# New places in SBUF for the activations and the split weights of a two-layer decoder trunk

## The chip, the core and the metric

The kernel runs on one NeuronCore of a Trainium2 chip. The metric is the time of one execution on the device in microseconds (us), as the median of several runs; less is better. The engines are called as the profile calls them: PE is TensorE's matmul side, PEld its side that loads weights, DVE is VectorE, ACT is ScalarE, POOL is GpSimd, SP is SyncE, which here issues all loads.

## The reference

Two layers, each on 256 rows of width 2048, all in float32:

```
u  = rms_norm(x);  z = u @ W_in          # 2048 -> 512 | 576 | 2048 | 2048 | 2048 | 2048
A  = latent attention, 16 heads, causal  # from the first two parts
R  = gelu(y) * rg_lru(conv4(x_b))        # from the next two
x += (sigmoid(g_a)*A + sigmoid(g_r)*R) @ W_out
x += relu(rms_norm(x) @ W_up)^2 @ W_down # 2048 -> 8192 -> 2048
x += sigmoid(rms_norm(x) @ W_pg) * (p @ W_pe)
```

and a last RMS norm. Nearly all arithmetic is in the dense products; W_up and W_down are the largest.

## The kernel before, in words

**Layout.** Features lie on the 128 partitions, the 256 rows of the sequence along the free dimension. `x` is [128, 16, 256]. The two big activation buffers `bufA` and `bufB` are [128, 16, 2, 256]: for each of 16 feature tiles a high and a low part of 256 values, 1024 bytes each.

**Weights.** The host lays all weights out as halves of [128, 1024] float32. `load` fetches a half into one of six `raw` buffers; `split_half` makes of it a rounded `hi` (ACT) and a remainder `lo` (DVE), both float32r, 4096 bytes in a partition. Three halves are held at a time: the pool `wsp` has three buffers for `hi` and three for `lo`, used in turn.

**Products.** Each product of two float32 numbers is made of three matmuls: hi times high part, hi times low part, lo times high part. `mm_both` walks 4 feature tiles of a half for two output tiles (24 matmuls per half), `mm_half` 8 feature tiles for one output tile (24 as well). In nearly all of them the 128x128 weights block is loaded anew before each matmul and 256 columns of the activations stream through. So PE's queue is an endless row of pairs, a load of 128 columns of weights and a matmul of 256 columns.

**Stages of a layer.** First the projections `c` and `kr`; then eight groups of two heads, each with `xb`, `yb`, `k`, `v`, `q`, `qr`, `lru`, `gr`, scores `s`, transposes `pt`, values `o`, and `ga`; then `out`; then four chunks of `up` and `down`, the MLP; then `pp` and `pg`. In `k`, `q`, `qr` and `lru` the moving operand is a smaller activation tile (`c0`, `c1`, `xc`); in `v` such a tile is the stationary operand and the split weights stream; in `s` and `o` both are small tiles.

**What sets the order.** One Python pass (`half`, `work`, `later`, `need`) writes the order of every engine out, from its own table of costs. The order does not depend on addresses.

**Addresses.** Pools are laid out one behind another in the order in which they are opened, each tile rounded up to 32 bytes; the first one begins at byte 16,512 of a partition. By the byte's remainder on division by 512 the tiles before stand so: `x`, `bufA`, `bufB`, `ident`, `ones` at 128; `raw`, `hi`, `lo`, the `tmp` tiles and `PT` at 192, in all buffers alike; the tiles of the pool `att` that are allocated behind `xbuf` (`c0`, `c1`, `k`, `q`, `v`, `xc`, `kr`, `qs` and others) at 224, since `xbuf` takes 2080 bytes. Blocks inside these tiles follow at multiples of 512 bytes. So 128 and 192 are multiples of 64, and 224 is a multiple of 32 alone.

Of the kernel before, what the change touches and what calls it, by code (L numbers as in the profile page):

```python
# [11 lines left out]
F32 = mybir.dt.float32  # L12
F32R = mybir.dt.float32r
# [5 lines left out]
P = 128  # L19
S = 256  # L20
D = 2048
KT = D // P
DEPTH = 2
# [21 lines left out]
NPC = _c  # L45
# [8 lines left out]
def _parts(x, bits, n):  # L54

    out = []
    x = Fraction(x)
    for i in range(n):
        if x == 0:
            out.append(0.0)  # L60
            continue
        b = bits if i < n - 1 else 24
        m, e = math.frexp(float(x))
        q = Fraction(2) ** (e - b)
        v = Fraction(round(x / q)) * q
        out.append(float(v))
        x -= v
    return out


def _centered(x):
    x = x - math.floor(x)
    return x - 1 if x > Fraction(1, 2) else x
# [3 lines left out]
def trunk_kernel(ctx: ExitStack, tc: tile.TileContext, xT, pT, pos, par, gfin, invf, wu, out):  # L77
    nc = tc.nc

    const = ctx.enter_context(tc.tile_pool(name="const", bufs=1))  # L80
    wraw = ctx.enter_context(tc.tile_pool(name="wraw", bufs=6))
    wsp = ctx.enter_context(tc.tile_pool(name="wsp", bufs=3))
    tmp = ctx.enter_context(tc.tile_pool(name="tmp", bufs=6))
    att = ctx.enter_context(tc.tile_pool(name="att", bufs=1))
    tiny = ctx.enter_context(tc.tile_pool(name="tiny", bufs=4))
    banks = {
        t: (ctx.enter_context(tc.tile_pool(name=f"ps_{t}", bufs=n, space=PSUM)), n)
        for t, n in (("mm", 3), ("s", 2), ("t", 1), ("o", 1), ("r", 1))
# [4 lines left out]
    def f(ap):  # L93
        return ap.bitcast(F32)
# [50 lines left out]
    def load_to(h):  # L145
        while nxt["dma"] <= min(h, n_halves - 1):
            load(nxt["dma"])
            nxt["dma"] += 1
# [6 lines left out]
    def split_half(h):  # L155
        load_to(h)
        src = raws.pop(h)
        hi = wsp.tile([P, 1024], F32R, tag="hi", name=f"hi{h}")
        lo = wsp.tile([P, 1024], F32R, tag="lo", name=f"lo{h}")
        A.activation(hi, src, AF.Copy)  # L160

        E["A"] = max(E["A"], E["P"]) + 0.95
        work(E["A"] + LATENCY - 0.3, E["A"])
        V.tensor_tensor(out=lo, in0=src, in1=f(hi), op=ALU.subtract)  # L164
        E["V"] = max(E["V"], E["A"] + LATENCY) + 1.14
        halves[h] = (hi, lo, E["V"] + LATENCY)
# [42 lines left out]
    def later(key, *steps, deps=(), rank=1, also=()):  # L209

        job = Job((key, *also), rank, deps, steps)
        at = len(jobs)
        while at and jobs[at - 1].rank > rank:
            at -= 1
        jobs.insert(at, job)
# [11 lines left out]
    def work(until_v, until_a):  # L227
        until = {"V": until_v, "A": until_a, "G": until_v}
        while True:
            best = None  # L230
            for j in jobs:
                at = j.start()
                if at is None:
                    continue
                eng = j.steps[0][0]
                idle = at - E[eng]
                if at < until[eng] and (idle < 0.02 or at < E["P"] + STALL) and (best is None or idle < best[0] - 0.02):
                    best = (idle, at, j)
                    if idle < 0.02:
                        break  # L240
            if best is None:
                return
            best[2].step(best[1])

    def half():
        h = nxt["used"]
        nxt["used"] += 1
        while nxt["half"] <= min(h + min(LA, max(h - 1, 0)), n_halves - 1):
            split_half(nxt["half"])
            nxt["half"] += 1  # L250
        load_to(h + PD)
        work(E["P"] + WINDOW + 0.9, E["P"] + WINDOW)
        hi, lo, at = halves.pop(h)
        E["P"] = max(E["P"], at)
        return hi, lo
# [86 lines left out]
        return tmp.tile([P, S], F32, tag="h", bufs=3, name=name)  # L342


    x = const.tile([P, KT, S], F32, name="x")

    bufA, bufB = (const.tile([P, KT, 2, S], F32R, name=n) for n in ("bufA", "bufB"))
    parT = const.tile([P, DEPTH * NPC], F32, name="parT")
    gf = const.tile([P, KT], F32, name="gf")
    nc.sync.dma_start(out=parT, in_=par)  # L350
    nc.sync.dma_start(out=x[:, 0:2, :], in_=xT[:, 0:2, :])
    load_to(0)
# [12 lines left out]
    make_identity(nc, ident)  # L365
    ones = const.tile([P, P], F32, name="ones")
    V.memset(ones, 1.0)
    power = const.tile([P, 4], F32, name="power")
    A.activation(power, ones[:, 0:4], AF.Copy, scale=-0.5)
    mask = const.tile([P, S], F32, name="mask")  # L370
    V.memset(mask[:, 0:P], 0.0)
# [2 lines left out]
    ropeS = const.tile([P, S], F32, name="ropeS")  # L374

    def rope_tables():
        fr = const.tile([P, 1], F32, name="invf")
        nc.sync.dma_start(out=fr, in_=invf)
        slots = []
        for n, tag in enumerate(("xch", "xcl", "vh", "vl")):  # L380
            w = att.tile([P, 512], F32, tag=tag, name=f"rope_w{n}")
            slots += [w[:, 0:S], w[:, S:512]]
        posi, ang, p2, p1, rem, turn, k, k2 = slots
        nc.sync.dma_start(out=posi.bitcast(I32), in_=pos.partition_broadcast(P))
        ops = []

        def ts(*a, **kw):
            ops.append(("V", 0.21, lambda: V.tensor_scalar(*a, **kw)))

        def tt(*a, **kw):  # L390
            ops.append(("V", 0.35, lambda: V.tensor_tensor(*a, **kw)))

        def rounded(o, src, by):
            ts(out=o, in0=src, scalar1=by, scalar2=ROUND, op0=ALU.mult, op1=ALU.add)
            ts(out=o, in0=o, scalar1=ROUND, scalar2=None, op0=ALU.subtract)

        def less(o, src, kk, c):
            ops.append(("V", 0.35, lambda: V.scalar_tensor_tensor(out=o, in0=kk, scalar=-c, in1=src, op0=ALU.mult, op1=ALU.add)))

        ops.append(("V", 0.21, lambda: V.tensor_copy(ang, posi.bitcast(I32))))  # L400
        ts(out=ang, in0=ang, scalar1=fr, scalar2=None, op0=ALU.mult)

        rounded(p2, ang, 2.0 ** -20)
        less(rem, ang, p2, 2.0 ** 20)
        rounded(p1, rem, 2.0 ** -10)
        less(rem, rem, p1, 2.0 ** 10)
        for n, (p, e) in enumerate(((p2, 20), (p1, 10))):
            c = _parts(_centered(Fraction(2) ** e / (2 * _PI)), 12, 3)
            if n == 0:
                ts(out=turn, in0=p, scalar1=c[0], scalar2=None, op0=ALU.mult)  # L410
            else:
                less(turn, turn, p, -c[0])
            rounded(k, turn, 1.0)
            less(turn, turn, k, 1.0)
            less(turn, turn, p, -c[1])
            less(turn, turn, p, -c[2])
        rounded(k, turn, 1.0)
        less(turn, turn, k, 1.0)
        c = _parts(2 * _PI, 12, 3)
        rounded(k2, rem, float(1 / (2 * _PI)))  # L420
        for v in c:
            less(rem, rem, k2, v)
        less(rem, rem, turn, -float(2 * _PI))
        rounded(k, rem, float(1 / (2 * _PI)))
        for v in c:
            less(rem, rem, k, v)
        ts(out=k, in0=rem, scalar1=3.1415925, scalar2=-3.1415925, op0=ALU.min, op1=ALU.max)

        ts(out=k2, in0=k, scalar1=-1.0, scalar2=None, op0=ALU.mult)
        tt(out=k2, in0=k, in1=k2, op=ALU.max)  # L430
        ts(out=k2, in0=k2, scalar1=-1.0, scalar2=math.pi / 2, op0=ALU.mult, op1=ALU.add)
        ops.append(("A", 1.0, lambda: A.activation(ropeS, k, AF.Sin)))
        ops.append(("A", 1.0, lambda: A.activation(ropeC, k2, AF.Sin)))

        for b in (0, 64):
            ts(out=ropeS[b:b + 32, :], in0=ropeS[b:b + 32, :], scalar1=-1.0, scalar2=None, op0=ALU.mult)
        later("rope", *ops, rank=1)


    cl = const.tile([P, DEPTH, 16], F32, name="cl")  # L440
    cl2 = const.tile([P, DEPTH, 16], F32, name="cl2")
    hba = const.tile([P, DEPTH, 16], F32, name="hba")
    hbx = const.tile([P, DEPTH, 16], F32, name="hbx")

    def lru_constants():
        work_ = t512("lru_c")
# [196 lines left out]

    PT = tuple(att.tile([P, 512], F32R, name=f"pt_{w}") for w in ("hi", "lo"))

    xbuf = att.tile([P, 2, 260], F32, name="xbuf")
    V.memset(xbuf[:, :, 0:4], 0.0)

    def split_steps(d, name, src, tag, cols=512):
# [35 lines left out]
    def mixer(l, u, mg, norm):  # L685
# [9 lines left out]
        for n in range(4):  # L695
            i, pr = divmod(n, 2)
            key = ("c", i, pr, l)
            ps = mm_pair(f"c{i}{pr}_{l}", key, u, hooks.get(n, ()))
            later(key, ("A", 0.6, lambda i=i, pr=pr, ps=ps: A.activation(dest(i, pr), ps, AF.Copy)), rank=-1)
            if l == n == 0:  # L700
                rope_tables()
                lru_constants()
            nl.squares((nl.name, "sq", n), lambda i=i, pr=pr: raw[i, pr], i, deps=(key,), last=pr == 1)
# [729 lines left out]
```

## Time and profile before

| what | value |
|---|---|
| median of 2 runs | 2882.11 us (2880.01 to 2884.22) |
| the profiled execution | 2881.91 us, of which 2880.1 us are the span of the profile |
| PE | 2853.1 us busy, 99% of the span, 24,800 matmuls |
| PEld | 2846.8 us busy, 99%, 24,800 loads of weights |
| DVE, ACT | 1861.3 us (65%) and 1538.4 us (53%) |
| DMA | 535.43 MB, mean 186 GB/s |

A matmul's duration in the profile reaches from its start to the end of its last column, and the next one starts long before that; what a stream of matmuls costs is read from the distance of their starts, which is called the pace below.

### The profile page before, as it was taken

What the parts mean: (1) busy time and instruction counts of PE and PEld (TensorE: products, weight loads), DVE (VectorE), ACT (ScalarE), POOL (GpSimd) and SP (SyncE); (2) the same over time, 40 slices, a digit from 0 to 9 for tenths busy, and PEclk for the clock granted to TensorE, in tenths of its full rate; (3) what the DMA queues carried; (4) which work ended last, traced back from release to release, by engine and by line L of the source; (5) the groups of instructions that cost most, each with busy time, mean ns of one, the idle gap of its engine ahead of it and who ended that gap; (6) DMA issues with size and microseconds to landing.
All of it is one profiled execution on the core that took longest, in us unless ns stands there. A gap on an engine that the chain in (4) does not pass through costs nothing.

```text
span 2880.1 us, 60564 instructions
## 1 busy us (share of the span) xinstructions
PE 2853.1 (99%) x24800; PEld 2846.8 (99%) x24800; DVE 1861.3 (65%) x2420; ACT 1538.4 (53%) x2050; POOL 10.1 (0%) x17
## 2 busy tenths in 40 slices
PE   8999999999999999999999999999999999999998
PEld 8999999999999999999999999999999999999998
DVE  7877777765555555556758777777555555555665
ACT  5666666644444443444546666666453444434555
POOL 0000000000000000000000000000000000000000
PEclk9999999999999999999999999999999999999999
DMA  6555555555555555655555555555555555555553
GB/s 232 169 176 179 172 171 178 178 184 190 197 193 194 195 193 195 198 195 191 190 188 172 176 169 176 176 178 179 186 191 195 194 196 193 194 194 197 196 187 129
DMA packets 272583, 535.43 MB, mean 186 GB/s; under 512 B 30512, under 2 KB 30768, under 8 KB 272304
## 3 DMA queue, kind: packets, MB, share of 16 engines
q1 hardware_dynamic: 272304, 531.55, 55.6%
q8 instruction: 194, 3.18, 0.4%
q14 instruction: 85, 0.70, 0.1%
HBM read 529.33 MB, written 2.10 MB: 185 GB/s over the span
## 4 chain that ended last, share of the span: by engine, by line
PE 98%; ACT 1%; DVE 0%; DMA 0%; issue 0%; SPq 0%; ACTq 0%; POOLq 0%
PE up L284 24%; PE down L284 21%; PE yb L284 6%; PE gr L284 6%; PE xb L284 6%; PE out L284 5%; PE pg L284 5%; PE ga L284 5%; PE c L284 3%; PE down L259 1%; PE down L260 1%; PE down L261 1%; PE o L1040 1%; PE s L984 1%; PE v L872 1%; PE v L873 1%
## 5 line engine op out<-in xcount | busy, mean ns | idle before, releaser
L160 ACT ACTIVATE hi<-raw 128x1024 fp32r<-128x1024 f32 x1004 | 1065.7, 1061 | 1311.6 <-DMA raw<-wu 467.4
L164 DVE TENSOR_TENSOR lo<-raw,hi 128x1024 fp32r<-128x1024 f32 x1004 | 1229.5, 1225 | 808.1 <-ACT hi L160 786.0
L284 PE MATMUL up<-bufA,hi 128*128 128x256 f32 x2048 | 316.2, 276 | 0.0
L284 PE MATMUL up<-bufB,hi 128*128 128x256 f32 x2048 | 316.2, 276 | 0.0
L284 PE MATMUL down<-bufB,hi 128*128 128x256 f32 x1792 | 276.0, 276 | 0.0
L284 PE MATMUL down<-bufA,hi 128*128 128x256 f32 x1792 | 276.0, 276 | 0.0
L284 PEld LDWEIGHTS up<-bufA,hi 128*128 128x128 f32 x2048 | 270.6, 188 | 0.1
L284 PEld LDWEIGHTS up<-bufB,hi 128*128 128x128 f32 x2048 | 270.6, 188 | 0.1
L284 PEld LDWEIGHTS down<-bufB,hi 128*128 128x128 f32 x1792 | 236.4, 188 | 0.0
L284 PEld LDWEIGHTS down<-bufA,hi 128*128 128x128 f32 x1792 | 236.4, 188 | 0.0
L284 PE MATMUL up<-bufA,lo 128*128 128x256 f32 x1024 | 199.7, 276 | 0.0
L284 PE MATMUL up<-bufB,lo 128*128 128x256 f32 x1024 | 199.6, 276 | 0.0
L284 PE MATMUL down<-bufA,lo 128*128 128x256 f32 x896 | 174.5, 276 | 0.0
L284 PE MATMUL down<-bufB,lo 128*128 128x256 f32 x896 | 174.4, 276 | 0.0
L284 PEld LDWEIGHTS up<-bufA,lo 128*128 128x128 f32 x1024 | 154.4, 188 | 0.0
L284 PEld LDWEIGHTS up<-bufB,lo 128*128 128x128 f32 x1024 | 154.3, 188 | 0.0
L284 PEld LDWEIGHTS down<-bufA,lo 128*128 128x128 f32 x896 | 134.9, 188 | 0.0
L284 PEld LDWEIGHTS down<-bufB,lo 128*128 128x128 f32 x896 | 134.8, 188 | 0.0
L284 PE MATMUL xb<-bufB,hi 128*128 128x256 f32 x512 | 81.4, 281 | 0.0
L284 PE MATMUL yb<-bufB,hi 128*128 128x256 f32 x512 | 81.3, 281 | 0.0
L284 PE MATMUL yb<-bufA,hi 128*128 128x256 f32 x512 | 81.3, 281 | 0.0
L284 PE MATMUL xb<-bufA,hi 128*128 128x256 f32 x512 | 81.3, 281 | 0.0
(563 smaller groups left out, 5630.8 us busy)
## 6 DMA issues: line engine op xcount, KB each, us to landing
raw<-wu SPq DMA_DIRECT2D x1744, 256.0 KB, 3.0
raw<-wu SPq DMA_DIRECT2D x132, 512.0 KB, 3.3
y<-rows SPq DMA_DIRECT2D x4, 512.0 KB, 4.0
x<-xT SPq DMA_DIRECT2D x3, 512.0 KB, 7.5
x<-xT SPq DMA_DIRECT2D x2, 256.0 KB, 4.3
praw<-pT SPq DMA_DIRECT2D x2, 256.0 KB, 4.0
parT<-par SPq DMA_DIRECT2D x1, 184.0 KB, 2.5
rope_w<-pos SPq DMA_DIRECT2D x1, 128.0 KB, 4.4
```

The lines of the kernel that those rows point to most:

```text
L160: A.activation(hi, src, AF.Copy)
L164: V.tensor_tensor(out=lo, in0=src, in1=f(hi), op=ALU.subtract)
L259: T.matmul(o, lhsT=wh, rhs=ah, start=start, stop=False, skip_group_check=shared)
L260: T.matmul(o, lhsT=wh, rhs=al, start=False, stop=False, skip_group_check=shared)
L261: T.matmul(o, lhsT=wl, rhs=ah, start=False, stop=stop, skip_group_check=shared)
L284: T.matmul(ps[:, t * S:(t + 1) * S], lhsT=w[:, (4 * t + kk) * P:(4 * t + kk + 1) * P], rhs=a, start=k == n == t == 0, stop=k == 15 and n = ...
L872: T.matmul(o, lhsT=ch, rhs=wh, start=k == 0, stop=False)
L873: T.matmul(o, lhsT=ch, rhs=wl, start=False, stop=False)
L984: T.matmul(o, lhsT=qr, rhs=kr["rot"][w][:, 0:n], start=False, stop=m == 1)
L1040: T.matmul(o[:, j * P:S], lhsT=v[:, j * S + t * P:j * S + (t + 1) * P], rhs=q[:, c], start=n == 0, stop=n == 5, skip_group_check=True,)
```

## The change

The pools are opened in another order and some tiles change pools. The tiles of odd sizes (`parT`, `gf`, `power`, `invf`, the four LRU constants, `xbuf`) move to a pool `small` that is opened first, with `tiny` behind it and a filler `even` of 32 bytes. Their sizes add up to 4480 bytes, so `const` begins at byte 20,992, which is 41 times 512. The pool `wsp` becomes three pools of one `hi` and one `lo` each, with fillers of 256, 128 and 64 bytes between them.

After it `x`, `bufA`, `bufB`, `ident`, `ones` and `raw` stand at remainder 0; the three pairs of `hi` and `lo` at 256, 384 and 448, by the number of the half modulo 3; and `tmp` and `att`, with `PT`, `c0`, `c1`, `k`, `q`, `v`, `xc`, `kr` and `qs`, at 448. Half h takes pair h modulo 3, as the turn of three buffers did before. No instruction is added, removed or moved.

```
+    small = ctx.enter_context(tc.tile_pool(name="small", bufs=1))
+    tiny = ctx.enter_context(tc.tile_pool(name="tiny", bufs=4))
+    even = ctx.enter_context(tc.tile_pool(name="even", bufs=1))
     const = ctx.enter_context(tc.tile_pool(name="const", bufs=1))
     wraw = ctx.enter_context(tc.tile_pool(name="wraw", bufs=6))
-    wsp = ctx.enter_context(tc.tile_pool(name="wsp", bufs=3))
+
+    wsp = []
+    for i, pad in enumerate((256, 128, 64)):
+        ctx.enter_context(tc.tile_pool(name=f"pad{i}", bufs=1)).tile([P, pad // 4], F32, name=f"pad{i}")
+        wsp.append(ctx.enter_context(tc.tile_pool(name=f"wsp{i}", bufs=1)))
...
-        hi = wsp.tile([P, 1024], F32R, tag="hi", name=f"hi{h}")
-        lo = wsp.tile([P, 1024], F32R, tag="lo", name=f"lo{h}")
+        hi = wsp[h % 3].tile([P, 1024], F32R, tag="hi", name=f"hi{h}")
+        lo = wsp[h % 3].tile([P, 1024], F32R, tag="lo", name=f"lo{h}")
...
+    even.tile([P, 8], F32, name="even")
...
-    parT = const.tile([P, DEPTH * NPC], F32, name="parT")
-    gf = const.tile([P, KT], F32, name="gf")
+    parT = small.tile([P, DEPTH * NPC], F32, name="parT")
+    gf = small.tile([P, KT], F32, name="gf")
...
-    xbuf = att.tile([P, 2, 260], F32, name="xbuf")
+    xbuf = small.tile([P, 2, 260], F32, name="xbuf")
```

## Rows read from the trace of the kernel before

**Rows 1.** The page: span, busy time, granted clock by slices, chain by engine.

```profile
span 2880.1 us, 60564 instructions
...
PE 2853.1 (99%) x24800; PEld 2846.8 (99%) x24800; DVE 1861.3 (65%) x2420; ACT 1538.4 (53%) x2050; POOL 10.1 (0%) x17
...
PEclk9999999999999999999999999999999999999999
...
PE 98%; ACT 1%; DVE 0%; DMA 0%; issue 0%; SPq 0%; ACTq 0%; POOLq 0%
```

**Rows 2.** PE's waits: who for whom, us in total, times, longest.

```profile
PE c L284 <- ACT hi L160: 8.6, 1, 8.6
```

**Rows 3.** Instructions by line: busy us, mean ns | idle before, releaser; the split.

```profile
L160 ACT ACTIVATE hi<-raw 128x1024 fp32r<-128x1024 f32 x1004 | 1065.7, 1061 | 1311.6 <-DMA raw<-wu 467.4
L164 DVE TENSOR_TENSOR lo<-raw,hi 128x1024 fp32r<-128x1024 f32 x1004 | 1229.5, 1225 | 808.1 <-ACT hi L160 786.0
```

**Rows 4.** Instructions by line: the matmuls of the MLP, three rows of eight.

```profile
L284 PE MATMUL up<-bufA,hi 128*128 128x256 f32 x2048 | 316.2, 276 | 0.0
...
L284 PE MATMUL down<-bufB,hi 128*128 128x256 f32 x1792 | 276.0, 276 | 0.0
...
L284 PE MATMUL up<-bufA,lo 128*128 128x256 f32 x1024 | 199.7, 276 | 0.0
```

**Rows 5.** Instructions by line: matmuls of other stages on the big buffers.

```profile
L284 PE MATMUL xb<-bufB,hi 128*128 128x256 f32 x512 | 81.4, 281 | 0.0
L284 PE MATMUL yb<-bufB,hi 128*128 128x256 f32 x512 | 81.3, 281 | 0.0
...
L284 PE MATMUL gr<-bufA,hi 128*128 128x256 f32 x512 | 79.4, 277 | 0.0
...
L284 PE MATMUL ga<-bufA,hi 128*128 128x256 f32 x448 | 71.6, 282 | 0.0
...
L284 PE MATMUL out<-bufB,hi 128*128 128x256 f32 x448 | 71.0, 281 | 0.0
...
L284 PE MATMUL xb<-bufB,lo 128*128 128x256 f32 x256 | 51.0, 281 | 0.0
...
L284 PE MATMUL ga<-bufA,lo 128*128 128x256 f32 x224 | 44.1, 278 | 0.0
```

**Rows 6.** Single tiles, duration in ns as min/median/max: matmuls of `k`, `v`.

```profile
L259 PE MATMUL k<-c1hi,hi x128: 277/280/281, 100.4 to 1939.7; 128*128 128x256 f32 x128
L872 PE MATMUL v<-hi,c1hi x128: 277/280/285, 103.2 to 1942.5; 128*128 128x256 f32 x128
```

**Rows 7.** Timeline of PE in the MLP: start us, us, instruction.

```profile
999.72 0.62 PE L284 MATMUL up<-bufA,hi 128*128 128x256 f32 x4
...
1001.76 0.62 PE L284 MATMUL up<-bufA,hi 128*128 128x256 f32 x4
```

**Rows 8.** Timeline of PE in `out`, layer 0.

```profile
600.05 0.63 PE L284 MATMUL out<-bufB,hi 128*128 128x256 f32 x4
...
602.17 0.63 PE L284 MATMUL out<-bufB,hi 128*128 128x256 f32 x4
```

**Rows 9.** Timeline of PE around the values of one group, inside `ga`.

```profile
364.58 0.39 PE L284 MATMUL ga<-bufA,lo 128*128 128x256 f32 x2
...
366.62 0.40 PE L284 MATMUL ga<-bufA,lo 128*128 128x256 f32 x2
366.85 0.28 PE L1040 MATMUL o<-pt_hi,v_4h 128*128 128x256 f32 x1
...
367.26 0.40 PE L1040 MATMUL o<-pt_lo,v_4h 128*128 128x256 f32 x2
...
369.66 0.63 PE L284 MATMUL ga<-bufA,hi 128*128 128x256 f32 x4
...
371.07 0.63 PE L284 MATMUL xb<-bufA,hi 128*128 128x256 f32 x4
```

**Rows 10.** Timeline of PEld in scores with 128 moving columns.

```profile
413.10 0.19 PEld L261 LDWEIGHTS s<-k_5h,q_5l 128*128 128x128 f32 x1
413.21 0.19 PEld L984 LDWEIGHTS s<-krk0h,qs 128*128 128x128 f32 x1
413.32 0.19 PEld L984 LDWEIGHTS s<-krk0l,qs 128*128 128x128 f32 x1
```

More of the change, by code (lines that the diff above doesn't have):

```diff
@@ L78, in trunk_kernel @@
     nc = tc.nc
+    small = ctx.enter_context(tc.tile_pool(name="small", bufs=1))
+    tiny = ctx.enter_context(tc.tile_pool(name="tiny", bufs=4))
+    even = ctx.enter_context(tc.tile_pool(name="even", bufs=1))
     const = ctx.enter_context(tc.tile_pool(name="const", bufs=1))
     wraw = ctx.enter_context(tc.tile_pool(name="wraw", bufs=6))
-    wsp = ctx.enter_context(tc.tile_pool(name="wsp", bufs=3))
+    wsp = []
+    for i, pad in enumerate((256, 128, 64)):
+        ctx.enter_context(tc.tile_pool(name=f"pad{i}", bufs=1)).tile([P, pad // 4], F32, name=f"pad{i}")
+        wsp.append(ctx.enter_context(tc.tile_pool(name=f"wsp{i}", bufs=1)))
     tmp = ctx.enter_context(tc.tile_pool(name="tmp", bufs=6))
     att = ctx.enter_context(tc.tile_pool(name="att", bufs=1))
-    tiny = ctx.enter_context(tc.tile_pool(name="tiny", bufs=4))
     banks = {
@@ L367, in trunk_kernel @@
     V.memset(ones, 1.0)
-    power = const.tile([P, 4], F32, name="power")
+    power = small.tile([P, 4], F32, name="power")
     A.activation(power, ones[:, 0:4], AF.Copy, scale=-0.5)
@@ L376, in rope_tables @@
     def rope_tables():
-        fr = const.tile([P, 1], F32, name="invf")
+        fr = small.tile([P, 1], F32, name="invf")
         nc.sync.dma_start(out=fr, in_=invf)
@@ L437, in rope_tables @@
         later("rope", *ops, rank=1)
[L440 to L443, printed above, removed]
+    cl = small.tile([P, DEPTH, 16], F32, name="cl")
+    cl2 = small.tile([P, DEPTH, 16], F32, name="cl2")
+    hba = small.tile([P, DEPTH, 16], F32, name="hba")
+    hbx = small.tile([P, DEPTH, 16], F32, name="hbx")
     def lru_constants():
```

## The prediction

> **What bounds the kernel now.** I read the page first. PE is busy for 2853.1 of 2880.1 us, the chain that ended last is 98% PE, and the granted clock is at full speed (the 2.4 GHz level) in all 40 slices [rows 1]. The list of PE's waits comes next: its longest is one wait of 8.6 us at the start, and no other line reaches 3 us [rows 2]. So PE never starves in the body. The makers of its weights have room: a half feeds 24 matmuls, 24 x 113 ns = 2.7 us, and its split takes 1061 ns of ACT and 1225 ns of DVE [rows 3]. The time is therefore the number of matmuls times their pace, and the question is only what the new places do to that pace.
>
> The pace comes from two views. In the list by line, matmuls of one shape (256 columns, a new 128x128 block each) have different mean durations: all eight rows of the MLP stand at 276 ns [rows 4], `xb`, `yb` and `out` at 281, `gr` at 277, `ga` between [rows 5]. The timeline gives the distance of starts. In the MLP 18 matmuls start within 1001.76 - 999.72 = 2.04 us, 113.3 ns each [rows 7]; in `out` 18 take 602.17 - 600.05 = 2.12 us, 117.8 ns each [rows 8]. No wait stands in either stretch, and the clock is the same. So 276 ns goes with a pace of 113.3 and 281 ns with 117.8: a fast and a slow pace, 4.5 ns apart.
>
> The slow pace is not a matter of remainders alone. Within one `ga`, on the same buffers at 128 and 192, 18 matmuls from 364.58 to 366.62 us take 113.3 ns each; then six value matmuls come, whose stationary tile stands at remainder 224; and behind them 12 matmuls from 369.66 to 371.07 us take 117.5 ns each [rows 9]. A stream keeps the pace into which it falls, until something odd interrupts it. Where one operand stands at 224, off a grid of 64 bytes, the fast pace is not reached at all: `k` and `v` have medians of 280 ns, and their fastest is 277 [rows 6]. My reading is that the two reading streams of PE, weights and activations, get in each other's way or not by their phase, that the phase depends on addresses, and that on the 64-byte grid both paces are stable. That is inferred; no row shows a read being held up.
>
> **The change, part by part.** Nothing is added, removed or moved in any queue, SP's and POOL's included, and no wait is added: the turn of three buffers stays, as h modulo 3. I cost the moves of `parT`, `gf`, the constants, `xbuf`, `x` and `raw` at nothing: they are operands of ACT, DVE and DMA. ACT and DVE have 1.7 and 1.5 us free in each half of 2.7 us, by the split alone; if an address cost them 0.1 us per instruction, that cover would still hold.
>
> What can move is the pace, and I sum what lies above the fast one, at 4.5 ns of pace for 5 ns of duration.
> 1. Off the grid now, on it afterwards (224 becomes 448, a multiple of 64): `k`, `v` and `q` with 384 matmuls each and `qr` with 192, 1344 in all, at 280 ns, so 3.5 ns over the fast pace [rows 6]: 1344 x 3.5 = 4.7 us.
> 2. On the grid, but slow now: `out` with two rows of 448 and two of 224, 1344 x 4.5 = 6.0 us; `xb` and `yb` with four rows each, 3072 matmuls at 281, 13.8 us; `ga` with two rows of 448 and two of 224, about half of it slow, 1344 x 2.2 = 3.0 us. Together 22.8 us [rows 5].
> 3. The MLP: `up` 6144 and `down` 5376 in these eight rows and 768 more by the code (the last pair of each chunk), 12,288 matmuls, all fast [rows 4]: nothing to gain there above 113.3 ns, and 12,288 x 4.5 = 55 us to lose.
>
> The ceiling by the paces seen is thus 4.7 + 22.8 = 27.5 us. The pace at the new distances between weights and activations (256, 384 and 448 bytes modulo 512 instead of 64) stands in no row. Its bounds are, below, the closest succession of loads of any row, 110 ns in the scores, where a matmul has only 128 columns [rows 10], and above, the slow pace of 117.8. I take 113.3 for it, the row with the most matmuls, since both operands stay on the 64-byte grid and the blocks inside a buffer already step by 512 bytes without any effect on that pace.
>
> For part 1 I take the whole 4.7 us. For part 2 I take 70%, 16 us: the slow pace of `xb`, `yb` and `out` begins behind value matmuls with an operand at 224, which will be at 448, so the entry changes; but which of two stable paces a stream falls into is not settled by that, and entries with odd instructions (transposes, the norm's one-column matmuls) remain. Sum: 4.7 + 16 = 21 us off. Against the profiled execution, 2881.9 us (2880.1 of span and 1.8 around it), that is 2861 us; the median of the runs, 2882.1, differs by 0.2 us.
>
> **Rivals.**
> *Places do not matter.* PE reads weights and activations without regard to where they lie, and the two paces come from what interrupts the stream. For it: one pair of remainders shows both paces [rows 9]. Against it: the rows of `k` and `v`, which never reach 276 [rows 6]. The time stays at 2882, within some 8 us. The Trainium skill speaks for it: "SBUF — State Buffer", section "Who interferes with whom", gives PE two independent read ports, one for the moving operand and one for weights, and has it that PE never waits on anyone. By that rule the sum of parts 1 and 2 is zero; here the trace does not agree in full, with 113.3 beside 117.8 ns and no wait in either.
>
> *The MLP loses its pace.* Its place is the stream of `up` and `down`. The distance of 64 bytes which is fast there now is given up, and a half in a slot with a bad distance runs at 117.8. One slot of three costs 55 / 3 = 18 us, and 6 us in `c`, `gr` and `pg` (3840 matmuls by the code, mostly fast now), less part 1: 2901. Two slots give 2925, all three 2949. It decides as soon as the MLP's mean pace rises by 21 us / 12,288 = 1.7 ns. For it: the slow pace, once entered, holds for a whole `out` [rows 5, 8], so an MLP that enters it would keep it too. Against it: part 3's argument on steps of 512 bytes.
>
> *The fast pace is not the floor.* If a distance exists at which the streams do not meet at all, a matmul could follow every 110 ns, as loads do in the scores [rows 10]. Nearly all of the 24,800 matmuls [rows 1] have 256 columns; at 3.3 ns each that is 80 us, beside the 27.5: 2774; with one slot of three, 2834. Against it: no row of 256 columns has a mean under 276 ns, whichever remainders it has. The Trainium skill has a rule for it in "TensorE: Matmul & The Clock Gate", section "Back-to-back issue gap": N/2.4 + 2.5 ns, 109.2 ns for 256 columns. By it the sum would be an estimate of 100 us under 113.3; the trace has nothing under 113.3 in a stream, so the rule has not held here so far.
>
> **How the numbers follow.** The forecast has 0.53 (2850 to 2875 by how much of part 2 comes); places without effect 0.17 (2874 to 2890); the MLP's loss 0.22 (2885 to 2949, evenly); the lower floor 0.08 (2774 to 2840). The predicted time is 2861. The range 2840 to 2915 holds the first two cases and half of the third, 0.81. A measurement of this kernel tells about 2% from no change, here 2824 and 2940. Faster by more than that needs the lower floor in two slots or more, 0.06; slower needs all three slots at the slow pace or worse, 0.07; within 2% is left with 0.87.
>
> **What would show it.** In the profile after: `up` and `down` still at 276 ns, with 113.3 ns between starts; `k`, `v`, `q` at 276 instead of 280; `xb`, `yb` and `out` mostly at 276. If these three stay at 281 while `k` drops, only part 1 came (2877). A mean of 279 or more in `up` is the second rival. A pace under 113 ns anywhere in `up` is the third, and my floor would be wrong. If all means stay, places do not matter. A pace that differs between three successive halves would show that distances beyond the grid of 64 bytes count, which I have denied.

## The result, and the profile after

The change made the kernel **slower**: 2975.53 us, median of two runs (2974.28 to 2976.79), against 2882.11; the ratio is 1.0324 [1.028, 1.0369]. The forecast was 2861 us with a range of 2840 to 2915, and no change beyond 2%.

The page of the kernel after, with the two lines of the split (busy us, mean ns | idle before):

```profile
span 2975.0 us, 60564 instructions
...
PE 2948.5 (99%) x24800; PEld 2943.9 (99%) x24800; DVE 1863.1 (63%) x2420; ACT 1536.9 (52%) x2050; POOL 10.1 (0%) x17
...
PEclk9999999999999999999999999999999999999999
...
PE 98%; ACT 1%; DMA 0%; DVE 0%; issue 0%; SPq 0%; ACTq 0%; POOLq 0%
...
L167 ACT ACTIVATE hi<-raw 128x1024 fp32r<-128x1024 f32 x1004 | 1063.5, 1059 | 1404.9 <-DMA raw<-wu 333.2
L171 DVE TENSOR_TENSOR lo<-raw,hi 128x1024 fp32r<-128x1024 f32 x1004 | 1229.7, 1225 | 868.7 <-ACT hi L167 860.2
```

PE's waits after (who for whom, us in total, times, longest):

```profile
PE c L291 <- ACT hi L167: 8.4, 1, 8.4
```

Beside [rows 1 to 3] nothing differs but PE: the same 60,564 instructions and 24,800 matmuls, the clock at full speed (the 2.4 GHz level) in every slice, the split at 1059 and 1225 ns where it was 1061 and 1225, the longest wait still the one at the start. PE is busy for 95.4 us more and the span is 94.9 us longer. So it is the pace, and the list by line says where (PE alone, shapes kept apart; line 291 was 284):

```profile
L291 PE MATMUL up<-bufA,hi 128*128 128x256 f32 x2048 | 326.7, 281 | 0.0
...
L291 PE MATMUL down<-bufB,hi 128*128 128x256 f32 x1792 | 285.6, 281 | 0.0
L291 PE MATMUL up<-bufA,lo 128*128 128x256 f32 x1024 | 204.4, 281 | 0.0
...
L291 PE MATMUL gr<-bufA,hi 128*128 128x256 f32 x512 | 82.0, 282 | 0.0
L291 PE MATMUL yb<-bufB,hi 128*128 128x256 f32 x512 | 82.0, 282 | 0.0
L291 PE MATMUL xb<-bufB,hi 128*128 128x256 f32 x512 | 82.0, 282 | 0.0
...
L291 PE MATMUL ga<-bufA,hi 128*128 128x256 f32 x448 | 73.1, 285 | 0.0
...
L291 PE MATMUL out<-bufB,hi 128*128 128x256 f32 x448 | 71.4, 281 | 0.0
```

Every row of the MLP went from 276 to 281 ns [rows 4]; `gr` from 277 to 282, `ga` from 282 to 285, while `xb`, `yb` and `out`, slow before, stayed at 281 to 282 [rows 5].

The view of single tiles (min/median/max of the duration in ns, first to last start in us) gives in its first starts the length of each stage. Of the kernel before, rows that were not shown:

```profile
L284 PE MATMUL out<-bufB,hi x448: 281/281/281, 551.3 to 630.1; 128*128 128x256 f32 x150
L284 PE MATMUL up<-bufA,hi x2048: 276/276/469, 641.7 to 1252.3; 128*128 128x256 f32 x187
L284 PE MATMUL pg<-bufA,hi x448: 276/276/471, 1342.5 to 1428.0; 128*128 128x256 f32 x150
```

and of the kernel after, with `k` and `v`, which answer to [rows 6]:

```profile
L266 PE MATMUL k<-c1hi,hi x128: 276/279/283, 105.1 to 1997.4; 128*128 128x256 f32 x128
...
L880 PE MATMUL v<-hi,c1hi x128: 278/281/283, 107.8 to 2000.2; 128*128 128x256 f32 x128
...
L291 PE MATMUL out<-bufB,hi x448: 274/281/287, 563.2 to 642.5; 128*128 128x256 f32 x150
L291 PE MATMUL up<-bufA,hi x2048: 274/281/468, 654.2 to 1292.5; 128*128 128x256 f32 x187
L291 PE MATMUL pg<-bufA,hi x448: 274/280/466, 1386.8 to 1475.4; 128*128 128x256 f32 x150
```

`k` and `v` had medians of 280 and stand at 279 and 281. From the first `up` to the first `pg` of layer 0, the MLP (with the few matmuls of `pp` behind it) took 1342.5 - 641.7 = 700.8 us before and 1386.8 - 654.2 = 732.6 after: 31.8 us more. Layer 1 lost 31.7 by its own rows. Taken the same way over both layers, the groups of heads lost 17.1 us, `c` with `kr` 5.5, `pg` 7.8, `out` 1.2. With 0.2 us gained at the start that is the 94.9 us of the span. Two thirds, 63.5 us, are the MLP, which the forecast had taken as safe.

The pace inside it, from the timeline of the kernel after (start us, us, instruction; only the runs of four are shown, every row of four is followed by one of two, so four such rows are a half of 24 matmuls):

```profile
1301.38 0.63 PE L291 MATMUL down<-bufB,hi 128*128 128x256 f32 x4
...
1304.20 0.64 PE L291 MATMUL down<-bufB,hi 128*128 128x256 f32 x4
...
1307.08 0.63 PE L291 MATMUL down<-bufB,hi 128*128 128x256 f32 x4
...
1309.92 0.63 PE L291 MATMUL down<-bufB,hi 128*128 128x256 f32 x4
...
1312.74 0.64 PE L291 MATMUL down<-bufB,hi 128*128 128x256 f32 x4
```

Three successive halves take 2.82, 2.88 and 2.84 us, that is 117.5, 120.0 and 118.3 ns per matmul (within 0.4, since the view prints hundredths of a us), and then it begins anew with 2.82. The mean of the three is 8.54 us / 72 = 118.6 ns, against 113.3 in [rows 7]: 12,288 x 5.3 = 65 us, which agrees with the 63.5 from the stages. None of the three halves has the fast pace, and one of the three paces, 120.0, is slower than any that the trace of before had shown in a settled stream. The pattern with a period of three halves is the one that the prediction named as proof that distances beyond the grid of 64 bytes count.

### The profile page after: what moved, and what is told of

It is laid out like the page before. It is cut to its first block, busy times and chain, and to the rows that moved or that the text cites. A ratio compares the mean times of both kernels' runs of the same rounds, so it can differ in the third digit from the quotient of the medians.

```text
span 2975.0 us, 60564 instructions
## 1 busy us (share of the span) xinstructions
PE 2948.5 (99%) x24800; PEld 2943.9 (99%) x24800; DVE 1863.1 (63%) x2420; ACT 1536.9 (52%) x2050; POOL 10.1 (0%) x17
## 4 chain that ended last, share of the span: by engine, by line
PE 98%; ACT 1%; DMA 0%; DVE 0%; issue 0%; SPq 0%; ACTq 0%; POOLq 0%
PE up L291 25%; PE down L291 21%; PE gr L291 6%; PE yb L291 6%; PE xb L291 6%; PE pg L291 5%; PE out L291 5%; PE ga L291 5%; PE c L291 3%; PE down L266 1%; PE down L268 1%; PE down L267 1%; PE o L1048 1%; PE s L992 1%; PE q L267 1%; PE v L880 1%
## 5 line engine op out<-in xcount | busy, mean ns | idle before, releaser
L167 ACT ACTIVATE hi<-raw 128x1024 fp32r<-128x1024 f32 x1004 | 1063.5, 1059 | 1404.9 <-DMA raw<-wu 333.2
L171 DVE TENSOR_TENSOR lo<-raw,hi 128x1024 fp32r<-128x1024 f32 x1004 | 1229.7, 1225 | 868.7 <-ACT hi L167 860.2
L291 PE MATMUL up<-bufA,hi 128*128 128x256 f32 x2048 | 326.7, 281 | 0.0
L291 PE MATMUL up<-bufB,hi 128*128 128x256 f32 x2048 | 326.7, 281 | 0.0
L291 PE MATMUL down<-bufA,hi 128*128 128x256 f32 x1792 | 285.7, 281 | 0.0
L291 PE MATMUL down<-bufB,hi 128*128 128x256 f32 x1792 | 285.6, 281 | 0.0
L291 PEld LDWEIGHTS up<-bufA,hi 128*128 128x128 f32 x2048 | 278.7, 189 | 0.1
L291 PEld LDWEIGHTS up<-bufB,hi 128*128 128x128 f32 x2048 | 278.7, 189 | 0.1
L291 PEld LDWEIGHTS down<-bufA,hi 128*128 128x128 f32 x1792 | 243.8, 189 | 0.0
L291 PEld LDWEIGHTS down<-bufB,hi 128*128 128x128 f32 x1792 | 243.8, 189 | 0.0
L291 PE MATMUL gr<-bufB,hi 128*128 128x256 f32 x512 | 82.0, 282 | 0.0
L291 PE MATMUL gr<-bufA,hi 128*128 128x256 f32 x512 | 82.0, 282 | 0.0
```

The lines of the kernel that those rows point to most:

```text
L291: T.matmul(ps[:, t * S:(t + 1) * S], lhsT=w[:, (4 * t + kk) * P:(4 * t + kk + 1) * P], rhs=a, start=k == n == t == 0, stop=k == 15 and n = ...
```

## The experiments

Below, **distance** is the address of the stationary block minus that of the streaming columns, modulo 512 bytes unless 256 is said. In the MLP it is the remainder of `hi` and `lo`, since `bufA` and `bufB` stand at 0. The theories: *distance* (each distance has its pace or paces), against *places* (the absolute remainder counts, or the pool layout as such), against *the turn* (three different remainders in succession disturb each other, while each alone would be fast). The small tiles are those of `att`, 448 in the kernel after. In all variants the instructions and their order are the same. Each time stands for a single execution, unless a number of executions is given; the kernel before took 2875 to 2883 us in the executions beside them, so differences of a few us between variants say little.

**One distance for all three pairs.** The first four runs put all three pairs at one remainder and leave everything else where the kernel after has it (a filler behind the pairs keeps `tmp` and `att` at 448):

```
-    for i, pad in enumerate((256, 128, 64)):
-        ctx.enter_context(tc.tile_pool(name=f"pad{i}", bufs=1)).tile([P, pad // 4], F32, name=f"pad{i}")
+    for i, pad in enumerate((64, 0, 0)):        # d256: 256, d384: 384, d448: 448
+        if pad:
+            ctx.enter_context(tc.tile_pool(name=f"pad{i}", bufs=1)).tile([P, pad // 4], F32, name=f"pad{i}")
         wsp.append(ctx.enter_context(tc.tile_pool(name=f"wsp{i}", bufs=1)))
+    ctx.enter_context(tc.tile_pool(name="tail", bufs=1)).tile([P, 96], F32, name="tail")   # 448 - pad bytes
```

> All three pairs of split weights at remainder 64, activations at 0 and small tiles at 448 as after the change: the distance from activations to weights is the 64 bytes of before. Theory D (the distance between the two streams of PE, modulo 512, sets the pace): MLP back at 113.3 ns, up at a mean of 276 ns, time 2850 to 2890. Theory A (absolute remainders count, and 0 is a bad one for the activations): MLP stays at 117 to 120 ns, time 2940 to 3000. Theory T (it is the turn of three different remainders that keeps the stream from settling): 113.3 ns, as theory D.

> All three pairs at 256. Theory D: what the first pair showed in the changed kernel, 119.6 ns, now everywhere: up at 282 to 283 ns, time near 2975 + 24,400 x (119.6 - 118.6) ns = 3000. Theory A: as the changed kernel, 2975. Theory T: one remainder for all, so the stream settles at 113.3 ns, 2850 to 2890.

> All three pairs at 384. Theory D: the second pair's 118.5 ns everywhere, up at 281 ns, time near 2972. Theory A: 2975. Theory T: 113.3 ns, 2850 to 2890.

> All three pairs at 448. Theory D: the third pair's 117.8 ns everywhere, up at 280 ns, time near 2956. Theory A: 2975. Theory T: 113.3 ns, 2850 to 2890.

Measured: 2893.51, 3000.15, 2971.87 and 2958.97 us, beside 2877.73 of the kernel before on the same chip. Single lines of the list by line (busy us, mean ns), first of the run at 64:

```profile
L293 PE MATMUL up<-bufA,hi 128*128 128x256 f32 x2048 | 316.2, 276 | 0.0
...
L293 PE MATMUL out<-bufB,hi 128*128 128x256 f32 x448 | 71.0, 281 | 0.0
...
L882 PE MATMUL v<-hi,c1hi 128*128 128x256 f32 x128 | 36.4, 285 | 0.0
```

of the run at 256:

```profile
L293 PE MATMUL up<-bufA,hi 128*128 128x256 f32 x2048 | 329.5, 283 | 0.0
...
L293 PE MATMUL out<-bufB,hi 128*128 128x256 f32 x448 | 72.0, 283 | 0.0
...
L882 PE MATMUL v<-hi,c1hi 128*128 128x256 f32 x128 | 35.4, 276 | 0.0
```

of the run at 384:

```profile
L293 PE MATMUL up<-bufA,hi 128*128 128x256 f32 x2048 | 326.7, 282 | 0.0
```

and of the run at 448:

```profile
L292 PE MATMUL up<-bufA,hi 128*128 128x256 f32 x2048 | 324.1, 279 | 0.0
```

The old distance of 64 gives the MLP its old 276 ns back, at new places. The other three make one slow stream each, with starts 120.0, 118.7 and 117.8 ns apart in the MLP; their mean, 118.8, is within 0.2 of the 118.6 of the kernel after. So the turn is not needed to explain it: each distance alone is slow. The time of the run at 64 lies 3.5 us above the 2850 to 2890 that *distance* gave it, and its `v`, at 285 ns, is slower than before; the small tiles are taken up below. And it is no matter of a stage: at 256 `out` has the 283 ns of `up`, while `v` in the same run, whose distance is 448 - 256 = 192, has 276.

**The other four distances.** The same edit with 192, 320, 128 and 0, to see the period:

> All three pairs at 192, a distance of 192 bytes. Theory D, with the distance alone in force whichever tile is the moving one: in the run at 256 the value projections had this distance (moving at 256, stationary at 448) and took 113.4 ns on 368 matmuls, so the MLP takes 113.3 ns, up at 276 ns, and the time is 2850 to 2880. Theory M (what the small tiles showed does not carry over to the big buffers): 117.8 or 120 ns, 2955 to 3000.

> A distance of 320 bytes. In the changed kernel k and q had it, k at 113.8 and q at 117.8 ns: two stable paces. Theory D: the MLP at either of the two as it enters, so 2850 to 2890 if both MLPs enter fast, 2905 with one of them slow, 2955 with all slow, and no pace between in a settled stretch. Theory M: 120 ns, near 3000.

> A distance of 128 bytes. In the run at 64 the projections k, q, qr had it (moving at 448, weights at 64) and took 119.0 ns in a turn of 115, 120 and 122. Theory D: the MLP at about 119 ns without a settled fast pace, up at 281 ns, time near 2977. Theory M: open, 113.3 possible, 2870.

> A distance of 0. In the run at 448 the projections had it and took 120.0 ns. Theory D: the MLP at 120.0 ns, up at 282 to 283 ns, time near 3000. Theory M: open, 113.3 possible, 2870.

Measured: 2959.41, 2895.18, 2969.88 and 2997.73 us, beside 2881.97. Of the run at 192, the list by line:

```profile
L293 PE MATMUL up<-bufA,hi 128*128 128x256 f32 x2048 | 324.1, 279 | 0.0
...
L293 PE MATMUL out<-bufB,hi 128*128 128x256 f32 x448 | 70.9, 280 | 0.0
...
L268 PE MATMUL k<-c1hi,hi 128*128 128x256 f32 x128 | 36.2, 283 | 0.0
```

and of the run at 0:

```profile
L293 PE MATMUL up<-bufA,hi 128*128 128x256 f32 x2048 | 329.5, 283 | 0.0
...
L268 PE MATMUL k<-c1hi,hi 128*128 128x256 f32 x128 | 35.5, 277 | 0.0
```

In pairs the eight runs repeat after 256 bytes: 0 and 256 take 2998 and 3000 us, 64 and 320 take 2894 and 2895, 128 and 384 take 2970 and 2972, 192 and 448 take 2959 and 2959. The small tiles confirm it in other places: `k` has the distance 192 - 448 = -256 in the run at 192, so 0 modulo 256, and there it has the 283 ns that `up` has in the run at 0; in the run at 0 its distance is -448, so 64, and it has 277. The match is not exact everywhere: at 128 `k` and `v` in `d64` start 119.6 and 119.9 ns apart, `up` in `d128` 118.7. At 320 the MLP is fast, but the time lies 5 us above the 2890 expected then, as at 64. The fast pace that was expected at 192 did not come; that miss is taken up below.

**Absolute places, and distances off the grid.** `s32` is `d64` with everything behind the filler `even` moved by 32 bytes, so that the activations stand at 32 and the pairs at 96, both off the grid of 64, at an unchanged distance. `d32` and `d96` move the pairs alone:

```
-    even.tile([P, 8], F32, name="even")
+    even.tile([P, 16], F32, name="even")        # s32, on top of d64
-    for i, pad in enumerate((64, 0, 0)):
+    for i, pad in enumerate((32, 0, 0)):        # d32, tail 416 bytes; d96: 96, tail 352 bytes
```

> The kernel with a distance of 64, all of it moved up by 32 bytes: activations at 32, weights at 96, small tiles at 480. Theory D256: nothing changes, MLP at 113.3 ns, 2893 us within 5. Theory G (each stream has to start on a grid of 64 bytes, as the prediction had it): neither does now, 117 to 118 ns everywhere, up at 280 ns, about 2950.

> A distance of 32 bytes, activations at 0. Theory D256 with a smooth course between its steps: between the paces of 0 and 64, and like the value projections before the change, which had it (118.2 ns): 118 ns, time near 2960. Theory S (steps of 64 bytes, so 32 counts as 0): 120.0 ns, 3000.

> A distance of 96 bytes. Theory D256, smooth: between 64 and 128, and with a course that repeats every 128 bytes it is like 224, which k and q had before the change (116.7 ns): time near 2925. Theory S: as 64, MLP at 113.3 ns, 2893.

Measured: 2892.69 (s32), 2970.9 (d32), 2968.16 (d96), beside 2882.31. The run with both operands off the grid, by line:

```profile
L293 PE MATMUL up<-bufA,hi 128*128 128x256 f32 x2048 | 316.2, 276 | 0.0
```

It is `d64` again, 276 ns and a time within 1 us. In the three placements tried (activations and pairs at 128 and 192 before, at 0 and 64 in `d64`, at 32 and 96 here) neither the place nor the grid of 64 bytes had an effect on the MLP; the distance is what counts. One more distance moved along, from `raw` to the split weights, since `raw` stands at the remainder of the activations in all variants; the kernel before rules it out, for there it was 0 (both at 192) with a fast MLP, and in `d0` it is 0 with the slowest.

`d32` and `d96` both have a mean of 281 ns in `up`. In `d32` the starts are 118.3 ns apart, close to the 118 that *distance* had expected, but the time is 11 us above the 2960. In `d96` neither of the two values expected came; 48 matmuls of `up` take 5.70 us, 118.7 ns each, while 42 of `out` in the same run take 4.93 us, 117.4 ns each (first and last row of each stretch):

```profile
1199.88 0.64 PE L293 MATMUL up<-bufA,hi 128*128 128x256 f32 x4
...
1205.58 0.63 PE L293 MATMUL up<-bufA,hi 128*128 128x256 f32 x4
```

```profile
600.17 0.63 PE L293 MATMUL out<-bufB,hi 128*128 128x256 f32 x4
...
605.10 0.63 PE L293 MATMUL out<-bufB,hi 128*128 128x256 f32 x4
```

Between 0 (120.0), 64 (113.3) and 128 (118.7) the pace does not run evenly.

**The small tiles moved to a good distance.** In `d64` the small tiles have 64 - 448 = -384, so 128 modulo 256, a bad one. `u64` is `d64` with a filler of 192 bytes in place of 384, so that they stand at 256, 192 away from the pairs:

```
-    ctx.enter_context(tc.tile_pool(name="tail", bufs=1)).tile([P, 96], F32, name="tail")
+    ctx.enter_context(tc.tile_pool(name="tail", bufs=1)).tile([P, 48], F32, name="tail")
```

> Activations at 0, all weights at 64, the small tiles and tmp at 256: every distance between the two streams outside the scores is 64 or 192 modulo 256, the two at which a pace of 113.3 ns has been seen. Theory D256 (distance modulo 256; at 64 and 192 two stable paces, 113.3 and 117.8 ns): no settled stretch at 119 or 120 ns; with both MLPs fast 2850 to 2890, each slow MLP 26 us more. Theory of a floor (distance 64 is fast everywhere once no small tile is at a bad distance): 2850 to 2857, below both kernels.

Measured: 2866.4 us (2865.73 to 2866.54, four executions), against 2882.31 of before; the ratio is 0.9944 [0.9927, 0.996]. By line:

```profile
L293 PE MATMUL up<-bufA,hi 128*128 128x256 f32 x2048 | 315.9, 276 | 0.0
...
L293 PE MATMUL out<-bufB,hi 128*128 128x256 f32 x448 | 69.0, 276 | 0.0
...
L882 PE MATMUL v<-hi,c1hi 128*128 128x256 f32 x128 | 35.4, 276 | 0.0
...
L268 PE MATMUL k<-c1hi,hi 128*128 128x256 f32 x128 | 35.3, 276 | 0.0
```

`k` and `v`, never at 276 in the kernel before [rows 6], are there, and with them `out`, whose own distance is the 64 that it had before [rows 5]: it stood at 281 there and in `d64`. So the prediction's reading of entries is borne out in general: the pace into which `out` falls depends on what streams ahead of it, and it changed when only the small tiles, and `tmp` with them, were moved. That the value matmuls decide it, as the prediction had it, is not shown: their two operands are both small tiles and kept their distance of 0 from `d64` to `u64`. Not every stream is fast in `u64`: `q` and `qr`, at a distance of 192, have 281 ns, and `gr`, behind them, 280.

**Is 192 slow, and does a bad half spoil its neighbours?** `d192` ran slow, though `v` at 192 had 276 ns in `d256`. Either 192 has no fast pace in the MLP, or it has both and `d192` fell into the slow one. In the kernel after, a half at 192 modulo 256 stands between halves at 128 and 0. Three runs, all with small tiles at 256:

```
-    for i, pad in enumerate((64, 0, 0)):
+    for i, pad in enumerate((64, 0, 128)):      # m192: pairs at 64, 64, 192; tail 64 bytes
+    for i, pad in enumerate((64, 0, 192)):      # m256: pairs at 64, 64, 256; no tail
+    for i, pad in enumerate((192, 0, 0)):       # u192: pairs at 192, 192, 192; tail 64 bytes
```

> As the kernel u64, but the third pair of weights at 192, the distance of the third pair of the changed kernel modulo 256. Theory B (192 has the fast pace too, and the MLP of the run at 192 had only fallen into the slow one): the stream comes fast out of two halves at 64 and stays at 113.3 ns in the third, time 2860 to 2880. Theory P (192 has 117.8 ns as its only pace on the big buffers): a third of the halves at 117.8, 8000 x 4.5 ns = 36 us more than u64, 2902, or more if the other two then fall slow (2955).

> As u64, but the third pair at 256, a distance that is 0 modulo 256. Theory H (each half has the pace of its own distance, and the fast pace is found again in the next half): a third at 119.6 ns, 8000 x 6.3 ns = 50 us more than u64, 2917. Theory C (a bad half throws the next ones out of the fast pace, into the slow one): 119.6 in one third and 117.8 in two, 16,000 x 4.5 = 72 us on top, 2985 at most.

> As u64 with all weights at 192. Theory B: two paces to choose from; which one the MLP takes is not foreseen, 2860 to 2890 when fast in both layers, 2955 when slow. Theory P: 117.8 ns everywhere, 2955.

Measured: 2862.22 (m192), 2967.53 (m256), 2943.05 (u192), beside 2882.18. The timeline of `m256` in the MLP, runs of four as above:

```profile
1302.34 0.63 PE L292 MATMUL down<-bufB,hi 128*128 128x256 f32 x4
...
1305.16 0.64 PE L292 MATMUL down<-bufB,hi 128*128 128x256 f32 x4
...
1308.04 0.64 PE L292 MATMUL down<-bufB,hi 128*128 128x256 f32 x4
...
1310.87 0.63 PE L292 MATMUL down<-bufB,hi 128*128 128x256 f32 x4
```

The half at 256 takes 2.88 us, 120.0 ns per matmul, and the halves at 64 before and behind it 2.82 and 2.83, 117.5 and 117.9: the slow pace of a distance which has the fast one in `u64`. One bad pair in three costs far more than a third: 2967.5 - 2866.4 = 101 us in all against the same kernel with all three at 64. In the MLP alone, from the first `up` to the first `pg` of layer 0, it is 731.8 us in `m256`, 700.3 in `u64` and 740.8 in `d0`, where all three are at 0: 31.5 us of 40.5, or three quarters.

`m192` differs from `m256` by the remainder of one pair alone, 192 for 256, and is 105 us faster. Its mean in `up` is 276 ns over all three pairs, so 192 does have the fast pace. `u192` shows that it need not come: with all three there `up` is at 279, as in `d192` and `d448`. The same run has both paces at 192, since `k` and `q` have that distance too (192 - 256 = -64): by the timeline the starts of `q` are 113.4 ns apart, those of `k` 117.8.

```profile
L268 PE MATMUL k<-c1hi,hi 128*128 128x256 f32 x128 | 35.8, 279 | 0.0
...
L268 PE MATMUL q<-c0hi,hi 128*128 128x256 f32 x128 | 35.4, 276 | 0.0
```

So both paces occur at 64 and at 192; none of the runs says what decides the entry.

**A version faster than both kernels.** `m192` again, with more executions:

> The version with pairs at 64, 64 and 192 and small tiles at 256, timed in rounds beside the kernel before, since its single time was the lowest. Theory B: as in its first look 2862 us, a ratio to before of 0.993, with up at 276 ns. If its stream had only fallen into the fast pace by chance, some executions would be 20 us or more longer.

```profile
L293 PE MATMUL up<-bufA,hi 128*128 128x256 f32 x2048 | 315.9, 276 | 0.0
...
L293 PE MATMUL gr<-bufA,hi 128*128 128x256 f32 x512 | 79.7, 278 | 0.0
...
L293 PE MATMUL out<-bufB,hi 128*128 128x256 f32 x448 | 69.0, 276 | 0.0
```

Measured: 2862.9 us (2862.31 to 2864.15, four runs), against 2876.16 of before on that chip: a ratio of 0.9951 [0.9935, 0.9968]. The interval lies below 1, though half a per cent is no change by the 2% of the forecast. None of the four executions was 20 us longer, so the stream fell into the fast pace each time. `m192` has the instructions of both kernels and differs from the kernel after by filler bytes alone, which are worth some 113 us. `u64`, with 0.9944, is faster than both as well; the times don't tell these two apart.

All distances in one table; the pace is the distance of starts in a settled stream of the MLP:

| distance, modulo 256 | runs | `up`, mean ns | pace, ns | time, us |
|---|---|---|---|---|
| 0 | d0, d256 | 283 | 120.0 | 2997.7, 3000.2 |
| 32 | d32 | 281 | 118.3 | 2970.9 |
| 64 | d64, d320, s32, u64 | 276 | 113.3 | 2893.5, 2895.2, 2892.7, 2866.4 |
| 64, beside halves at 0 | m256 | 282 (all three) | 117.7 | 2967.5 |
| 96 | d96 | 281 | 118.7 | 2968.2 |
| 128 | d128, d384 | 282 | 118.7 | 2969.9, 2971.9 |
| 192 | d192, d448, u192 | 279 | 117.8 | 2959.4, 2959.0, 2943.1 |
| 192, beside halves at 64 | m192 | 276 (all three) | 113.3 | 2862.2 |

## Why the prediction was wrong

**What bounds the kernel** held: PE at 99%, no wait to speak of behind the start, the clock at its upper level in every slice, and the whole loss in the distance of starts. So did the two stable paces at the distance of 64, with 276 ns for 113.3 and 281 for 117.8 as the sign to read them by. The sign does not carry over to other distances: in `d192` the pace of 117.8 goes with 279 ns, and 281 or 282 go with 118.3 and 118.7 in `d32`, `d96` and `d128`. (Of the twelve slow matmuls read in one `ga` [rows 9], the last six are of `xb`; their pace is as read.)

**The step that failed** is the pace put on the new distances, behind part 3: "I take 113.3 for it, the row with the most matmuls, since both operands stay on the 64-byte grid and the blocks inside a buffer already step by 512 bytes without any effect on that pace." The second reason is true and says only that 512 is a period; it is, and so is 256. Nothing in it covers 256, 384 and 448 against 64; these took 120.0, 118.7 and 117.8 ns each by itself (`d256`, `d384`, `d448`), and 118.6 on the mean in the kernel after, which is the 63.5 us lost in the MLP. The first reason took the grid for the cause, from `k` and `v` alone [rows 6]: they were off the grid, and they were also at distances of -32 and +32. `s32` separates the two: off the grid at a distance of 64 the MLP keeps 276 ns. In the trace of before all the fast streams had one distance, 64, and that should have been read as a sample of one. The upper bound for the unknown distances was wrong as well: "above, the slow pace of 117.8" was the slowest that rows showed at 64, and four of the eight distances on the grid gave more, 118.7 and 120.0. The lower bound, 110 ns, was not the closest succession of loads in that trace either: three loads of the transposes `pt` start at 544.64, 544.71 and 544.82 us. Only the price of the third rival hung on it.

**Part 1**, 4.7 us off for `k`, `v`, `q` and `qr`: not found. `k` went from 280 to 279 and `v` from 280 to 281. They did land on the grid, but one of the three pairs, at 448, then stood at a distance of 0 from them, the worst. In `u64` `k` and `v` came to 276, `q` and `qr` to 281.

**Part 2**, 16 us off for `xb`, `yb`, `ga` and `out`: none of it came; `ga` lost 3 ns more. That an entry can turn the pace was right, as `u64` shows, where `out` went to 276, though not by the value matmuls' own distance; but an entry helps only a distance that has a fast pace, and between halves at 0 and 128 none kept it.

**Part 3**, nothing: it cost 63.5 us, and `c`, `kr` and `pg` 13.3 more.

**The rivals.** *The MLP loses its pace* is what happened, with a chance of 0.22. Its price for three slots was 2949, and 2975.5 came. Against that sum the MLP was 63.5 instead of 55 us, since its paces reach 120.0, and everything else lost 94.9 - 63.5 = 31.4 us where the sum had 18 - 4.7 = 13.3: together 8.5 + 18.1 = 26.6 us. Its rule that the slots add up, 18 us each in the MLP, was wrong too: in `m256` one bad slot cost 63 us there and 101 us in all. Nor do the chances fit together: 0.22 spread evenly from 2885 to 2949 leaves 0.03 above 2940, where 0.07 was given for slower. *Places do not matter* fell: the same instructions take from 2862 to 3000 us by filler bytes alone. The Trainium skill's rule in "SBUF — State Buffer", section "Who interferes with whom", that PE never waits on anyone, with an independent read port for weights and one for the moving operand, does not account for that: the pace goes from 113.3 to 120.0 ns by the distance of the two operands, with no wait on another engine in the stretches compared. *The fast pace is not the floor* fell as far as it was tried: no settled stream of 256 columns in any run had a pace under 113.3 ns, at any of the ten distances. The 109.2 ns of the Trainium skill, "TensorE: Matmul & The Clock Gate", section "Back-to-back issue gap", an estimate from its formula, were not reached; but the section gives that formula for a matmul by itself and says that in a stream of loads and matmuls both set the spacing, so it was no rule for this stream, and 113.3 says nothing against it.

**What stays open.** The table is measured, the mechanism is not: that the two reading streams of PE meet with a period of 256 bytes would give such a table, but no row shows a read being held up. Why 64 and 192 have two paces (96 as well, 118.7 in `up` and 117.4 in `out`), and what decides between them at an entry (`k` against `q` in `u192`, `out` in `d64` against `u64`), was not settled; only that in `m256` the halves at 64 next to one at 0 run at the slow one.

## What to carry to other kernels

Where PE is the bound and the profile shows no wait, read the distance of starts and compare one shape's mean duration over all tiles; a difference of 5 ns in 276 was worth 63.5 us in the MLP here. A pace that all fast rows have at one distance between two operands says nothing of another distance: change one filler, measure eight remainders, and only then lay the pools out. Check every pair of operands that meet on PE, small tiles included, since one bad stream can also take the fast pace from the good ones beside it.

## What was not expected of the hardware

- The pace of pairs of a load and a matmul of 256 columns depends on the distance of the two operands in a partition, modulo 256 bytes: in the MLP 120.0 ns at 0, 118.7 at 96 and 128, 118.3 at 32, and 113.3 or 117.8 at 64 and 192.
- Which pace a distance has can hang on the halves next to it, and it holds over a whole MLP of some 700 us per layer: halves at 64 took 117.7 ns beside one at 0 in `m256` and 113.3 in `u64`; at 192 the MLP was slow in all three runs with 192 alone and fast beside halves at 64 in `m192`.
- Remainders that are equal modulo 256, which the change gave the activations and every third pair, are the worst case measured, 120.0 ns.
